# Placing the first projection's products between the transposes of x, and asking for the rotation tables behind the first weights

## The chip, the cores and the metric

The kernel runs on 1 core of one Trainium2 chip. The metric is the device time in microseconds (us) of that core. Before the change, three runs gave a median of 2097.58 us (2097.52 to 2098.06). All names of engines are those of the profile: PE (TensorE, the matrix engine, with PEld for its loads of the stationary operand), DVE (VectorE), ACT (ScalarE), POOL (GpSimd) and SP (SyncE, which issues all DMAs here).

## The reference

One decoder block on x of 2048 rows by 1024 columns, all in float32:

```
h    = rmsnorm(x, norm_g)                         # per row
proj = h @ w_in                                   # 1024 -> 7680 columns
glu_in, conv_gate, q, k, v, attn_gate, merge = split(proj)
c      = silu(layernorm(depthwise_conv31(a * sigmoid(b))))    # a, b = halves of glu_in
y_conv = (c * silu(conv_gate)) @ w_conv_out
q, k   = rope(q), rope(k)                         # rotation by cos, sin tables
y_attn = (window_attention(q, k, v, sinks) * silu(attn_gate)) @ w_attn_out
x      = x + (sigmoid(m1) * y_conv + sigmoid(m2) * y_attn) @ w_out
out    = rmsnorm(x, final_norm_g)
```

The change touches only the very beginning: the norm of the first 1024 rows, their transposes, and the first products with `w_in`.

## The kernel before, in words

The rows are worked in two sweeps of 1024 rows, each sweep in two halves of 512. A sweep projects its rows (`project`), runs the convolution on DVE and the attention beside the projections, and then does the three output products. A float32 product is made of three products in the matrix engine's reduced form: every operand is split in a high part and a remainder ("lo"), and for each of the 8 slices k of the 1024 inputs PE does whi x h-high, whi x h-lo and wlo x h-high ("a triple", 128x512 each), summed in one PSUM bank over 24 products. `load_w` brings a weight tile in two parts (`raw_..0` for k = 0 to 3, `raw_..1` for k = 4 to 7): SP loads `raw`, ACT casts the high part `whi` (line 251), POOL subtracts for `wlo` (line 240).

The start of the first sweep is special. `load_first` asks for four row blocks of x (`xf`, 128x1024 each). `build_h_first` then, for each block, squares and sums it on ACT (line 347), takes a square root on ACT (348), a reciprocal (350) and a scaling of the block (351) on DVE. Then, for each k, it transposes four 128x128 pieces on PE into one PSUM bank `tpf_k` (line 358), copies the high part to `hT_k` on ACT (360) and the remainder on DVE (361). There are three such PSUM banks. `hT_0_k` are the eight tiles of the first half, `hT_1_k` those of the second.

The first items are `gb` and `ga` (the b and the a of glu) and `ka` (a k tile), each first on half 0 and later on half 1. `gb` half 0 is called `mm_gb_000` with weights `whi_gb_000`, `whi_gb_001`. In the kernel before, all of `build_h_first(0)` is run out first, that of half 1 is started on the `Line`, and then the products come. `Line` is the planner of PE's order: `spend(us)` advances a planned time after each triple, and a chain that has yielded `(us, latency)` goes on when its time is due, so that the transposes of half 1 fall between triples.

PE's order is the program's. The order on ACT, DVE, POOL and SP is set by the scheduler of the tile framework, but each of these engines then works its list strictly from the top. The rotation tables `cs` (two loads of 512 KB) are first read by DVE when the first k product is ready (line 457).

Of the kernel before, what the change touches and what calls it, by code (L numbers as in the profile page):

```python
# [52 lines left out]
def hybrid_block(ctx: ExitStack, tc: tile.TileContext, x, par_d, w_in, w_conv, sinks, w_attn, w_out,  # L53
# [16 lines left out]
    def f(ap):  # L70
        return ap.bitcast(F32)
# [8 lines left out]
    def slot(tag, shape, dt, name):  # L80
        n = int(np.prod(shape[1:]))
        full = HALO + T + 2 if tag in WIDE else 1024
        t = slots.tile([P, full], dt, tag=tag, name=name)
        v = t[:, 0:n]
        if len(shape) == 3:
            v = v.rearrange("p (a b) -> p a b", b=shape[2])
        elif len(shape) == 4:
            v = v.rearrange("p (a b c) -> p a b c", b=shape[2], c=shape[3])
        return v
# [11 lines left out]
    def load_first(half):  # L101
        xs = []
        for j in range(4):
            r0 = (4 * half + j) * P
            xs.append(slot(A[7 * half + j], [P, D], F32, f"xf{half}_{j}"))
            nc.sync.dma_start(out=xs[-1], in_=x2[r0:r0 + P, :])
        return xs

    x_first = load_first(0)
# [122 lines left out]
    line = Line()  # L232
# [63 lines left out]
    def make_tiles(tags, half, name):  # L296
        return [slot(tags[half * 8 + k], [P, 2, TH], F32R, f"{name}{half}_{k}") for k in range(KC)]
# [43 lines left out]
    def build_h_first(half, xs):  # L341

        ss = work.tile([P, 2, 4], F32, tag="ss0", name=f"ssf{half}")
        for j in range(4):
            xt = xs[j]
            sq = slot(C[j], [P, D], F32, f"sqf{half}_{j}")
            act.activation(out=sq, in_=xt, func=AF.Square, accum_out=ss[:, 0, j:j + 1])
            act.activation(out=ss[:, 1, j:j + 1], in_=ss[:, 0, j:j + 1], func=AF.Sqrt, bias=eps,
                           scale=1.0 / D)
            dve.reciprocal(out=ss[:, 0, j:j + 1], in_=ss[:, 1, j:j + 1])  # L350
            dve.tensor_scalar(out=xt, in0=xt, scalar1=ss[:, 0, j:j + 1], scalar2=None, op0=ALU.mult)
        yield 0.0, 6.0
        if half == 1:
            ht[1] = make_tiles(h_tags[0], 1, "hT0_")
        for k in range(KC):
            tp = tp_ps.tile([P, 4, P], F32, tag="tp", name=f"tpf{half}_{k}")
            for j in range(4):
                pe.transpose(out=tp[:, j, :], in_=xs[j][:, k * P:(k + 1) * P], identity=ident)
            d = ht[half][k].rearrange("p a (j t) -> p a j t", t=P)
            act.activation(out=d[:, 0], in_=tp, func=AF.Copy, scale=g_norm[:, k, :])  # L360
            dve.scalar_tensor_tensor(out=d[:, 1], in0=tp, scalar=g_norm[:, k, :], in1=f(d[:, 0]),
                                     op0=ALU.mult, op1=ALU.subtract)
            yield 0.44, 0.8

    def program():
        for s in range(NSWEEP):
            yield from sweep(s)

    def sweep(s):
# [36 lines left out]
        def glu_items(c):  # L406
            def ev_b(half, ps):
                if half == 0:
                    glu[c] = slot(glu_slot[c], [P, HALO + T], F32, f"glu{s}_{c}")
                    pool.tensor_copy(out=glu[c][:, 0:HALO], in_=glu_halo[:, c, :])  # L410
                o = HALO + half * TH
                act.activation(out=glu[c][:, o:o + TH], in_=ps, func=AF.Sigmoid)  # L412

            def ev_a(half, ps):
                g = glu[c][:, HALO + half * TH:HALO + (half + 1) * TH]
                dve.tensor_tensor(out=g, in0=ps, in1=g, op=ALU.mult)
                if half == 1:
                    if s + 1 < NSWEEP:
                        pool.tensor_copy(out=glu_halo[:, c, :], in_=glu[c][:, T:T + HALO])
                    line.bg.extend(conv_ops(c))  # L420

            return [project(w_in[C_GLU_B // P + c], h_rhs, f"gb{s}_{c}", ev_b),
                    project(w_in[C_GLU_A // P + c], h_rhs, f"ga{s}_{c}", ev_a)]
# [22 lines left out]
        def load_rope():  # L446
            for half in range(2):
                cs[half] = slot(AT[11 + half], [P, 2, TH], F32, f"cs{s}_{half}")
                t0 = s * T + half * TH
                nc.sync.dma_start(out=cs[half], in_=rope_t[:, :, t0:t0 + TH])  # L450
# [303 lines left out]
        nqkv = len(others)  # L754
        others += gates
        glu_after = list(GLU_AFTER)
        load_rope()
        if s == 0:
            halves = [item[2]() for item in glu_items(0) + others[:1]]
            halves[0][0][0]()  # L760
            xs = load_first(1)
            for _ in build_h_first(0, x_first):
                pass
            line.start(build_h_first(1, xs))
            for half in range(2):
                for i, item in enumerate(halves):
                    yield ((lambda: None) if half == i == 0 else item[half][0],) + item[half][1:]
            glu_after.pop(0)
        for i, item in enumerate(others):
            todo = [item] if s or i else []  # L770
# [183 lines left out]
```

## Time and profile before

| | |
|---|---|
| runs, median (range) | 2097.58 us (2097.52 to 2098.06) |
| profiled execution, its time / its span | 2100.21 us / 2098.5 us |
| busy: PE, PEld, DVE, ACT, POOL | 98%, 80%, 66%, 48%, 23% |
| the chain that ended last, by engine | PE 79%, DVE 11%, DMA 3%, ACT 3%, issue 2%, POOL 1% |
| first transpose / first product / PE without a pause from | 8.41 / 17.84 / 24.93 us |

The execution is a long stretch of PE work, with short waits. The share of PE in the whole span says little on this change, since it acts within the first 45 us only. There one reads the engines' lists in order of time, and asks of each instruction what it waited for.

### The profile page before, as it was taken

How to read it: one execution, taken by the hardware profiler on the slowest of the kernel's cores; microseconds unless marked ns; L12 is line 12 of the kernel's file. 1: busy time of each engine (PE TensorE's matmuls, PEld its weight loads, DVE VectorE, ACT ScalarE, POOL GpSimd, SP SyncE). 2: the span in 40 equal slices, each digit the busy share in tenths (PEclk: the TensorE clock that was granted, in tenths of full speed). 3: DMA queues.
4: the chain of work that ended last, by engine and by line, in shares of the span. 5: the costliest groups of instructions: out<-in, count | busy, mean ns of one | idle time of the engine just before them, and what ended most of it. 6: DMA issues, size and time to landing. Idle time of an engine off the chain costs nothing.

```text
span 2098.5 us, 27434 instructions
## 1 busy us (share of the span) xinstructions
PE 2049.7 (98%) x9256; PEld 1673.3 (80%) x9256; DVE 1394.8 (66%) x1901; ACT 1012.8 (48%) x2251; POOL 477.9 (23%) x336
## 2 busy tenths in 40 slices
PE   7999999999999999999999999999999999999998
PEld 6787887787778877788888888888888888888887
DVE  4979769899988347223558596698889944341224
ACT  6221366665666645112442214767667774521222
POOL 2445432343333322233001121111111110000200
PEclk9999999999999999999999999999999999999999
DMA  7345644554545874646343456555555577574432
GB/s 253 131 141 161 193 145 148 158 164 144 161 138 178 266 231 148 223 136 231 99 151 127 137 178 186 174 172 170 170 156 171 167 228 260 169 233 146 139 122 80
DMA packets 265819, 355.89 MB, mean 170 GB/s; under 512 B 28112, under 2 KB 126544, under 8 KB 265680
## 3 DMA queue, kind: packets, MB, share of 16 engines
q1 hardware_dynamic: 265680, 354.16, 53.1%
q8 instruction: 73, 1.20, 0.3%
q14 instruction: 66, 0.54, 0.1%
HBM read 234.51 MB, written 119.54 MB: 169 GB/s over the span
## 4 chain that ended last, share of the span: by engine, by line
PE 79%; DVE 11%; DMA 3%; ACT 3%; issue 2%; POOL 1%; SPq 1%; DVEq 0%; ACTq 0%; POOLq 0%
PE mm_ma L279 9%; PE o L874 8%; PE mm_yc L279 8%; PE mm_ya L279 7%; PE mm_ag L279 7%; PE mm_gb L279 7%; PE mm_mc L279 7%; DVE cv L390 6%; PE mm_ga L279 6%; PE mm_cg L279 6%; PE mm_q_b L279 3%; PE mm_q_a L279 3%; PE sc L563 2%; PE ov L611 2%; PE mm_v L279 1%
## 5 line engine op out<-in xcount | busy, mean ns | idle before, releaser
L390 DVE SCALAR_TENSOR_TENSOR cv<-glu,par,cv 128x1024 f32<-128x1024 f32 x480 | 682.5, 1422 | 6.3
L602 POOL TENSOR_SCALAR_AFFINE_SELECT pc<-pt 128x1024 fp32r<-128x1024 f32 x60 | 102.4, 1707 | 430.0 <-DVE pt L240 428.2
L874 PE MATMUL o<-wo,mT 128*128 128x512 f32 x768 | 181.3, 394 | 0.0
L874 PEld LDWEIGHTS o<-wo,mT 128*128 128x128 f32 x768 | 143.0, 188 | 32.1
L279 PE MATMUL mm_cg<-hT,whi_cg 128*128 128x512 f32 x512 | 163.3, 400 | 4.5 <-ACT glu L412 2.6
L279 PE MATMUL mm_ma<-hT,whi_ma 128*128 128x512 f32 x512 | 163.2, 400 | 3.9 <-ACT glu L412 3.9
L279 PE MATMUL mm_ga<-hT,whi_ga 128*128 128x512 f32 x512 | 162.5, 399 | 3.5 <-ACT ag L431 2.9
L279 PE MATMUL mm_ya<-aT,whi_ya 128*128 128x512 f32 x512 | 159.1, 392 | 3.4 <-DVE mp L788 3.4
L279 PE MATMUL mm_gb<-hT,whi_gb 128*128 128x512 f32 x512 | 160.8, 395 | 1.5 <-ACT ag L431 1.2
L279 PE MATMUL mm_ag<-hT,whi_ag 128*128 128x512 f32 x512 | 160.9, 395 | 1.2 <-ACT glu L412 1.2
L279 PE MATMUL mm_mc<-hT,whi_mc 128*128 128x512 f32 x512 | 161.1, 396 | 0.0
L279 PE MATMUL mm_yc<-uT,whi_yc 128*128 128x512 f32 x512 | 159.4, 392 | 0.0
L279 PEld LDWEIGHTS mm_ya<-aT,whi_ya 128*128 128x128 f32 x512 | 95.8, 188 | 25.6 <-DVE mp L788 3.1
L279 PEld LDWEIGHTS mm_ga<-hT,whi_ga 128*128 128x128 f32 x512 | 95.1, 190 | 25.3 <-ACT ag L431 3.3
L279 PEld LDWEIGHTS mm_cg<-hT,whi_cg 128*128 128x128 f32 x512 | 95.2, 191 | 25.1 <-ACT glu L412 3.1
L279 PEld LDWEIGHTS mm_ma<-hT,whi_ma 128*128 128x128 f32 x512 | 95.3, 191 | 24.4 <-ACT glu L412 4.3
L279 PEld LDWEIGHTS mm_mc<-hT,whi_mc 128*128 128x128 f32 x512 | 96.7, 189 | 22.4 <-ACT mc L431 0.4
L279 PEld LDWEIGHTS mm_yc<-uT,whi_yc 128*128 128x128 f32 x512 | 96.2, 188 | 21.8
L279 PEld LDWEIGHTS mm_gb<-hT,whi_gb 128*128 128x128 f32 x512 | 94.5, 188 | 22.2 <-ACT ag L431 1.7
L279 PEld LDWEIGHTS mm_ag<-hT,whi_ag 128*128 128x128 f32 x512 | 94.1, 188 | 21.1 <-ACT glu L412 1.6
L581 ACT ACTIVATE ss<-ss,st 128x128 f32<-128x128 f32 x256 | 99.8, 391 | 21.1 <-DVE st L576 20.5
L614 ACT COPY ss<-ov 64x256 f32<-64x256 f32 x128 | 47.0, 367 | 119.9 <-DVE ss L615 97.5
(363 smaller groups left out, 4328.1 us busy)
## 6 DMA issues: line engine op xcount, KB each, us to landing
qk<-d_q SPq DMA_DIRECT2D x256, 64.0 KB, 2.7
d_a<-ss SPq DMA_DIRECT2D x128, 128.0 KB, 1.9
aT<-d_a SPq DMA_DIRECT2D x32, 512.0 KB, 5.9
qk<-d_k SPq DMA_DIRECT2D x240, 64.0 KB, 2.2
raw_gb<-in_w_in_dram SPq DMA_DIRECT2D x34, 256.0 KB, 3.8
raw_ga<-in_w_in_dram SPq DMA_DIRECT2D x34, 256.0 KB, 3.2
raw_ag<-in_w_in_dram SPq DMA_DIRECT2D x32, 256.0 KB, 3.7
d_ag<-ag SPq DMA_DIRECT2D x32, 256.0 KB, 2.4
```

Of the source, the lines that this page charges most:

```text
L279: pe.matmul(out=ps, lhsT=a, rhs=b, start=(k == 0 and i == 0), stop=(k == KC - 1 and i == 2))
L390: dve.scalar_tensor_tensor(out=cv[c], in0=glu[c][:, j:j + T], scalar=tap(c, j), in1=cv[c], op0=ALU.mult, op1=ALU.add)
L563: pe.matmul(out=o, lhsT=q[:, h, :], rhs=r, start=(j == 0), stop=(j == 1))
L581: act.activation(out=sb[:, h, :], in_=sb[:, h, :], func=AF.Exp, scale=SCALE, bias=ngm[:, h:h + 1], accum_out=den[:, h:h + 1])
L602: pool.affine_select(out=pc, in_=f(pt), pattern=[[0, 2], [0, GQ], [1, P]], compare_op=ALU.is_ge, fill=0.0, base=0, channel_multiplier=-1)
L611: pe.matmul(out=ov, lhsT=vv, rhs=pp[:, i % 2], start=(i == 0), stop=(i == nm - 1))
L614: act.copy(oT[own], ovp[other, :, r, :])
L874: pe.matmul(out=ps, lhsT=a[:, c0:c0 + P], rhs=r, start=(k == 0 and i == 0), stop=(k == KC - 1 and i == 2))
```

## The change

Two things. The rotation tables are asked for after the first `gb` weights and the second half's rows, and no longer ahead of them. And for the first half of the rows, the transposes are no longer all done before the first triple: after tiles 0 and 1, one tile's transposes stand between two triples of `gb` (a generator is advanced by one step after each triple). The second half's preparation starts on the planner's line with a delay of 10 instead of 6 planned us.

```
@@ build_h_first
-        yield 0.0, 6.0
+        yield 0.0, 10.0
         if half == 1:
             ht[1] = make_tiles(h_tags[0], 1, "hT0_")
         for k in range(KC):
...
@@ sweep
-        load_rope()
-        if s == 0:
+        if s:
+            load_rope()
+        else:
             halves = [item[2]() for item in glu_items(0) + others[:1]]
             halves[0][0][0]()
             xs = load_first(1)
-            for _ in build_h_first(0, x_first):
-                pass
-            line.start(build_h_first(1, xs))
+            load_rope()
+
+            def first_blocks():
+                gen = build_h_first(0, x_first)
+                for _ in range(3):
+                    next(gen)
+                line.start(build_h_first(1, xs))
+                for us in halves[0][0][1]():
+                    yield us
+                    next(gen, None)
+
             for half in range(2):
                 for i, item in enumerate(halves):
-                    yield ((lambda: None) if half == i == 0 else item[half][0],) + item[half][1:]
+                    yield (lambda: None, first_blocks) if half == i == 0 else item[half]
             glu_after.pop(0)
```

How this stands in the engines' lists. From the 123rd row of PE's list on, and from about the 50th of the other engines', the two kernels' lists are the same.

PE, where tile 2's transposes and the first triple of `gb` meet. Before, tile 7's transposes are followed by the triples one after the other:

```order
L358 MATMUL tpf_7_227<-ident_r,xf_0_80 128x128
L358 MATMUL tpf_7_227<-ident_r,xf_1_82 128x128
L358 MATMUL tpf_7_227<-ident_r,xf_2_84 128x128
L358 MATMUL tpf_7_227<-ident_r,xf_3_86 128x128
L279 MATMUL mm_gb_000_267<-hT_0_0_124,whi_gb_000_139 128x512 x2
L279 MATMUL mm_gb_000_267<-hT_0_0_124,wlo_gb_000_140 128x512
L279 MATMUL mm_gb_000_267<-hT_0_1_125,whi_gb_000_139 128x512 x2
L279 MATMUL mm_gb_000_267<-hT_0_1_125,wlo_gb_000_140 128x512
```

Now, after tile 1's transposes, on the same engine:

```order
L279 MATMUL mm_gb_000_225<-hT_0_0_124,whi_gb_000_135 128x512 x2
L279 MATMUL mm_gb_000_225<-hT_0_0_124,wlo_gb_000_136 128x512
L358 MATMUL tpf_2_229<-ident_r,xf_0_80 128x128
L358 MATMUL tpf_2_229<-ident_r,xf_1_82 128x128
L358 MATMUL tpf_2_229<-ident_r,xf_2_84 128x128
L358 MATMUL tpf_2_229<-ident_r,xf_3_86 128x128
L279 MATMUL mm_gb_000_225<-hT_0_1_125,whi_gb_000_135 128x512 x2
L279 MATMUL mm_gb_000_225<-hT_0_1_125,wlo_gb_000_136 128x512
```

The triple of tile k now stands between the transposes of tile k+1 and those of tile k+2, up to the triple of tile 5; those of tiles 6 and 7 follow without a transpose. The first four transposes of half 1 come after the seventh triple of `ga`, where they came after its first.

ACT, the stretch after its work on the first row blocks. Before (`sqf` with `xf_..149` to `xf_..155` are the squares of half 1's row blocks):

```order
L251 CAST whi_gb_000_139<-raw_gb_000_137 128x512
L251 CAST whi_gb_001_145<-raw_gb_001_143 128x512
L360 ACTIVATE hT_0_4_128<-tpf_4_206,par 128x512
L360 ACTIVATE hT_0_5_129<-tpf_5_213,par 128x512
L360 ACTIVATE hT_0_6_130<-tpf_6_220,par 128x512
L347 ACTIVATE sqf_0_235,ssf_234<-xf_0_149 128x1024
L360 ACTIVATE hT_0_7_131<-tpf_7_227,par 128x512
L348 ACTIVATE ssf_234<-ssf_234,eps_t 128x1
L347 ACTIVATE sqf_1_240,ssf_234<-xf_1_151 128x1024
L347 ACTIVATE sqf_2_245,ssf_234<-xf_2_153 128x1024
L348 ACTIVATE ssf_234<-ssf_234,eps_t 128x1 x2
L347 ACTIVATE sqf_3_250,ssf_234<-xf_3_155 128x1024
```

Now, from the first square of half 1 on (its blocks are here `xf_..145` to `xf_..151`):

```order
L347 ACTIVATE sqf_0_205,ssf_204<-xf_0_145 128x1024
L348 ACTIVATE ssf_204<-ssf_204,eps_t 128x1
L360 ACTIVATE hT_0_2_126<-tpf_2_229,par 128x512
L347 ACTIVATE sqf_1_210,ssf_204<-xf_1_147 128x1024
L360 ACTIVATE hT_0_3_127<-tpf_3_239,par 128x512
L348 ACTIVATE ssf_204<-ssf_204,eps_t 128x1
L347 ACTIVATE sqf_2_215,ssf_204<-xf_2_149 128x1024
L347 ACTIVATE sqf_3_220,ssf_204<-xf_3_151 128x1024
L348 ACTIVATE ssf_204<-ssf_204,eps_t 128x1 x2
L360 ACTIVATE hT_0_4_128<-tpf_4_249,par 128x512
L360 ACTIVATE hT_0_5_129<-tpf_5_260,par 128x512
L251 CAST whi_ga_000_159<-raw_ga_000_157 128x512
```

All four squares of half 1 now stand ahead of `hT_0_4`, where three of them stood behind `hT_0_7`. The two casts of `whi_gb` moved ahead of `hT_0_0`; the casts of `whi_ga` stand between `hT_0_5` and `hT_0_7`. DVE's list follows: three of the four scalings of half 1's blocks stand ahead of the remainder of `hT_0_5`, the fourth right ahead of it.

SP's list of DMA issues. Before:

```order
L135 DMA par<-in_par_dram 128x280
L450 DMA cs_0_133<-in_rope_dram 128x2x512
L450 DMA cs_1_135<-in_rope_dram 128x2x512
L248 DMA raw_gb_000_137<-in_w_in_dram 128x512
L248 DMA raw_gb_001_143<-in_w_in_dram 128x512
L106 DMA xf_0_149<-in_x_dram 128x1024
```

Now, from the same row on:

```order
L135 DMA par<-in_par_dram 128x280
L248 DMA raw_gb_000_133<-in_w_in_dram 128x512
L248 DMA raw_gb_001_139<-in_w_in_dram 128x512
L106 DMA xf_0_145<-in_x_dram 128x1024
L106 DMA xf_1_147<-in_x_dram 128x1024
L106 DMA xf_2_149<-in_x_dram 128x1024
L106 DMA xf_3_151<-in_x_dram 128x1024
L450 DMA cs_0_153<-in_rope_dram 128x2x512
L450 DMA cs_1_155<-in_rope_dram 128x2x512
L248 DMA raw_ga_000_157<-in_w_in_dram 128x512
```

The two tables went behind the second half's rows and still stand ahead of `raw_ga`.

## Rows read from the trace of the kernel before

**Rows 1.** Busy time by stretch: stretch, its length, engines, granted clock, DMA.

```profile
11.09:17.84 6.75, 6.25 (x29) 5.05 (x30) 4.23 (x6) 5.62 (x10) 2.28 (x2) 1.00 1.04 404
17.84:25.60 7.76, 7.12 (x34) 5.30 (x33) 5.81 (x11) 7.73 (x17) 2.23 (x3) 1.00 0.63 241
```

**Rows 2.** PE's list by time: start, us, engine, line, out<-in, count, [idle <-releaser].

```profile
11.09 5.83 PE L358 MATMUL tpf<-ident_r,xf 128*128 128x128 f32 x25 [0.95 <-DVE xf L351]
17.84 0.71 PE L279 MATMUL mm_gb<-hT,whi_gb 128*128 128x512 f32 x2
23.58 0.73 PE L279 MATMUL mm_ga<-hT,whi_ga 128*128 128x512 f32 x2
24.93 0.50 PE L279 MATMUL mm_ga<-hT,wlo_ga 128*128 128x512 f32 x1 [0.62 <-POOL wlo_ga L240]
```

**Rows 3.** Chain of waits, the first 60 us: start, us, what.

```profile
3.72 8.00 DMA cs<-in_rope_dram
...
11.73 8.44 DMA raw_ga<-in_w_in_dram
...
25.43 0.44 PE tpf L358 x4
...
39.37 5.58 PE mm_gb L279 x24
```

**Rows 4.** ACT's list by time, in the columns of rows 2.

```profile
11.60 0.69 ACT L360 ACTIVATE hT<-tpf,par 128x512 fp32r<-128x512 f32 x1 [1.55 <-PE tpf L358]
...
14.87 1.13 ACT L251 CAST whi_gb<-raw_gb 128x512 fp32r<-128x512 f32 x2
15.89 1.85 ACT L360 ACTIVATE hT<-tpf,par 128x512 fp32r<-128x512 f32 x3
17.61 1.07 ACT L347 ACTIVATE sqf<-xf 128x1024 f32<-128x1024 f32 x1
...
18.66 0.70 ACT L360 ACTIVATE hT<-tpf,par 128x512 fp32r<-128x512 f32 x1
...
21.49 0.49 ACT L348 ACTIVATE ssf<-ssf,eps_t 128x1 f32<-128x1 f32 x2
...
22.90 0.62 ACT L251 CAST whi_ga<-raw_ga 128x512 fp32r<-128x512 f32 x1
```

**Rows 5.** SP's list of issues, and below it par's time to landing.

```profile
3.23 0.44 SPq L135 DMA_DIRECT2D par<-in_par_dram  x1
...
DMA to landing us min/median/max: 6.8/6.8/6.8
```

**Rows 6.** The transposes alone, in two stretches: count, ns min/median/max, from, to.

```profile
L358 PE MATMUL tpf<-ident_r,xf x7: 417/417/417, 13.6 to 14.9; 128*128 128x128 f32 x7
...
L358 PE MATMUL tpf<-ident_r,xf x3: 272/273/332, 17.4 to 17.7; 128*128 128x128 f32 x3
```

**Rows 7.** A later wait, PE's list by time.

```profile
197.78 1.08 PE L279 MATMUL mm_q_b<-hT,whi_q_b 128*128 128x512 f32 x2 [3.43 <-DVE rb_q__1_1524 L464]
...
199.09 1.06 PE L279 MATMUL mm_q_b<-hT,whi_q_b 128*128 128x512 f32 x2
...
200.37 1.06 PE L279 MATMUL mm_q_b<-hT,whi_q_b 128*128 128x512 f32 x2
```

**Rows 8.** The same stretch by windows: length, PE busy, granted clock, DMA.

```profile
198.00:201.00 3.00, 3.00 (x8) 0.50 0.47 158
202.00:204.00 2.00, 2.00 (x10) 1.00 0.82 244
```

**Rows 9.** DVE's list by time: remainders of hT, and scalings of half 1's blocks.

```profile
16.62 2.07 DVE L361 SCALAR_TENSOR_TENSOR hT<-tpf,par,hT 128x512 fp32r<-128x512 f32 x3 [0.86 <-ACT hT L360]
...
22.03 0.75 DVE L351 TENSOR_SCALAR xf<-xf,ssf 128x1024 f32<-128x1024 f32 x1
...
23.95 1.48 DVE L351 TENSOR_SCALAR xf<-xf,ssf 128x1024 f32<-128x1024 f32 x1
```

**Rows 10.** POOL's list by time.

```profile
23.60 2.98 POOL L240 TENSOR_TENSOR wlo_ga<-raw_ga,whi_ga 128x512 fp32r<-128x512 f32 x2 [5.53 <-ACT whi_ga L251]
```

## The prediction

> **What bounds the kernel now.** I read the busy time by stretch first, then the lists of PE, ACT, DVE, POOL and SP over the first 45 us, then the chain of waits. PE bounds the kernel, but not before 25 us. It transposes from 11.09 and starts the first triple only at 17.84 [rows 2]. In that stretch of 6.75 us PE looks busy (6.25) and ACT has 5.62; in the next, 7.76 us long, ACT has 7.73: there ACT's list never stops [rows 1]. PE waits a last time in this start for `wlo_ga`, whose cast stands on ACT behind three squares of half 1 (22.90, [rows 4]): the first two products of `ga` run from 23.58, the third only from 24.93 [rows 2]. So the start is bound by ACT as much as by PE, and the question for the change is when ACT delivers the tiles `hT`.
>
> Since the lists of all engines agree after the first 45 us, I take a delay at the end of the start as passed on in full: in the chain, PE's work follows without a gap from 25.43 to `gb` at 39.37 [rows 3].
>
> **The prices.** A triple costs 5.58 / 8 = 0.70, one tile's four transposes 0.44 beside triples [rows 3]. ACT, from start to start: a high part 0.58 ((1.85 - 0.69) / 2), a pair of casts 1.02 (14.87 to 15.89), a square with its read-out 1.05 (17.61 to 18.66), a root 0.2 [rows 4]. A high part is ready after 0.7. DVE: a remainder 0.66 from one to the next, ready after 0.75; a scaling 0.75 [rows 9].
>
> PE's early work costs more. The transposes take 417 ns each up to 14.9 and start 0.21 apart (7 in 1.3 us), so 0.85 per tile; after 17.4 they take 273 [rows 6]. The granted clock in the rows reads 1.00 in both stretches [rows 1], so it doesn't show this. It does at 198: after a wait of 3.43 us PE runs at 0.50 of its 2.4 GHz, and a triple takes 200.37 - 199.09 = 1.28 instead of 0.70; later it is 1.00 again [rows 7, 8]. I take 1.2 GHz from the first transpose to about 17, as before, since PE starts at the same 11.09 and has about as much to do.
>
> The Trainium skill, "TensorE: Matmul & The Clock Gate" (What's actually happening), says that half rate is the state in which PE starts, and that activity lifts it; the durations agree with that, the granted clock of the first rows doesn't.
>
> **The tables behind the weights.** `par` lands at 3.23 + 6.8 = 10.03 [rows 5]. The first table, 512 KB, landed next, at 3.72 + 8.00 = 11.72 [rows 3]. Now the two `raw_gb` parts, 512 KB together, stand there: I take 10.9 and 11.7. Earliest would be both at about 10.0 to 10.5, latest as before, when the casts began at 14.87 [rows 4]. The second half's blocks come 1 MB earlier, some 2.6 us at 400 GB/s [rows 1]; `raw_ga` has the same bytes ahead of it, and keeps its 11.73 + 8.44 = 20.2 [rows 3]. `cs` is read by DVE only after the first `ka`, past 35 us: its later landing, below 20, costs nothing.
>
> **The transposes and triples, step by step** (PE, then ACT and DVE where they are late):
> - Casts at 10.9 and 11.7, then `hT_0_0` at 12.2 (11.60 before, [rows 4]), ready 12.9, and `hT_0_1` at 12.8, the first square at 13.35.
> - Triple 0 starts at 12.93, waits for its remainder (13.7), and ends at 14.6: 4.9 us earlier than triple 0 did (17.84 plus its length). This is the gain of the change. Transposes of tile 2 to 15.4, triple 1 to 16.7, tile 3 to 17.6, all at half clock.
> - ACT: `hT_0_2` at 15.7, second square 16.3, `hT_0_3` 17.85, root, third square 18.6, fourth 19.7, two roots, and only then `hT_0_4` at 21.1. Here the gain goes back: before, `hT_0_4` stood at 15.89 [rows 4].
> - PE has triples 2 and 3 and the transposes of tiles 4 and 5 done at 20.25, and idles until 21.84. DVE makes the remainder of tile 4 at 22.05 to 22.8, behind the scaling of the third block. Triple 4 ends 23.3, tile 6 is transposed by 23.7, triple 5 waits for its remainder (24.2) and ends 24.6, tile 7's transposes end at 25.1.
> - `hT_0_7` at 25.26 (18.66 before), its remainder at 26.76, and triple 7 ends at 27.2. With three PSUM banks and two tiles of lead, each triple from the fourth on pays for part of the round from PE to ACT to DVE and back.
> - The first triple of `ga` follows with no wait (its casts at 22.3 and 24.5, POOL done by 24.4 with the first, 1.49 each [rows 10]), to 27.9.
>
> Before, PE had `gb`, the first triple of `ga` and four transposes of half 1 behind it at 24.93 + 0.23 + 0.44 = 25.60 [rows 2, 3]. The same work is done at 27.9 + 0.44 = 28.35. That is +2.75 us. The table loads and `glu` on ACT lie behind this and beside PE's `ga`: hidden. The transposes of half 1's last three tiles now fall between triples of `gb` half 1; the last triple there comes 1.4 us after the last transposes, whose high part and remainder take 0.3 + 0.7 + 0.75: about 0.2 more. Sum +2.95.
>
> On the profiled execution this is 2100.21 + 2.95 = 2103.2. It stood 2.63 above the median of the runs, which gives **2100.5 us**.
>
> Bounds of the unknown: by the same list, weights at 10.0 to 10.5 give +2.3, weights and blocks of half 1 as late as before +4.6; full clock from the start +1.5, half clock to the end of this `gb` +5.7.
>
> **A lock that may add to it.** The fourth scaling took 1.48 instead of 0.75 when it started at 23.95 behind a POOL subtraction begun at 23.60 [rows 9, 10]. Now it starts at 22.7 and POOL's first subtraction for `ga` at 22.9: a race by 0.2. If POOL is first, the scaling waits for POOL's 24.4, and the remainders of tiles 5 to 7 with it: +1.4. If DVE is first, nothing.
>
> The Trainium skill, "SBUF — State Buffer" (SBUF: two separate sides), calls the port pair that VectorE and GpSimd share an exclusive lock, held for a whole instruction. The row of 1.48 agrees. By this rule the sum is +2.95 or +4.35, by who comes first.
>
> **Rivals.**
> 1. *The interleave pays* (faster). ACT is early with every tile, and PE never waits from 11.09 on. For: PE idles in both stretches, and the first triple starts 4.9 us earlier. PE would need 33 transposes and 27 products, 8.25 x 0.44 + 9 x 0.70 = 9.9, and 2.7 more for the 5.4 us at half clock: done at 23.7, against 25.6. That is -1.9: 2095.7, at the very best. Against: the squares ahead of `hT_0_4` in ACT's list. It decides whether `hT_0_4` starts before about 17.5.
> 2. *Nothing moves* (within 0.5 of 2097.6). The wait for `ga`'s weights goes, the one for `hT` comes, and both are of a size. For: ACT's total work up to `glu` is the same in both kernels. Against: before, ACT's work for half 1 lay beside triples that had all they needed; now triples wait behind it.
> 3. *POOL takes the lock first*: +4.35, 2101.9. By the times above DVE is first by 0.2, which is less than I can place.
> 4. *The clock stays at half* through the first `gb`, since PE now has gaps: +5.7, 2103.3. Against: the gaps in my list are below 2 us, and the fall in the later stretch followed 3.43 us of idleness [rows 7, 8].
>
> By the page on the clock gate an idle stretch takes PE back to half rate; that rule would lead to rival 4, if the gaps were long enough.
>
> **How the numbers follow.** Forecast (2099.3 to 2101.5) 0.53, rival 1 0.10, rival 2 0.14, rival 3 0.15, rival 4 0.08. A measurement can tell about 0.2%, or 4.2 us, from no change. Rival 1 doesn't reach that at its best, so faster gets 0.02, for what I have not seen. Slower by more than 4.2 us needs 2101.8: rival 4, most of rival 3, and a little of the forecast's tail with late weights, 0.23. The rest, 0.75, is no difference. Range: from 2098.0, which takes in part of rival 2, to 2102.8, past rival 3 and short of rival 4.
>
> **What would show it.** In the profile after: the `whi_gb` casts from 10.9 to 12.3; the first triple's start near 12.9; `hT_0_4` on ACT at about 21, behind four squares; PE waiting for `hT` of ACT and DVE several times between 17 and 27, and no longer for `wlo_ga`; the first `ga` triple at about 27. The fourth scaling's time, 0.75 or 1.48, decides rival 3; transposes of 273 ns or of 417 ns after 18 decide rival 4. I am wrong if `hT_0_4` comes early, if the `raw_gb` parts land after 13, or if a wait after 45 us, where the lists agree, grows or shrinks by more than 1 us.

## The result, and the profile after

| | before | after |
|---|---|---|
| median of 20 runs each (range) | 2097.27 us (2095.51 to 2099.85) | 2100.49 us (2098.09 to 2102.95) |
| profiled execution, time / span | 2100.21 / 2098.5 us | 2102.25 / 2100.5 us |
| 4th row block's first transpose | 11.09 us | 12.03 us |
| first product of `ga` | 23.58 us | 28.68 us |
| first product of `kb` | 55.96 us | 60.18 us |

The ratio is 1.0017, 95% interval 1.001 to 1.0023: 3.2 us slower, where +2.9 was forecast.

Two times serve as marks below: the start of the first transpose that reads the fourth row block, which waits for nothing of the change, and the start of the first `kb` product, behind everything that the change touches. The distance between them I call the **start length**. It is 44.87 us before and 60.18 - 12.03 = 48.15 after, +3.28.

PE's list of the kernel after, in the columns of rows 2:

```profile
12.03 1.33 PE L358 MATMUL tpf<-ident_r,xf 128*128 128x128 f32 x5 [0.89 <-DVE xf L351]
13.28 1.58 PE L279 MATMUL mm_gb<-hT,whi_gb 128*128 128x512 f32 x2
...
15.79 0.93 PE L279 MATMUL mm_gb<-hT,whi_gb 128*128 128x512 f32 x2
...
19.32 0.50 PE L279 MATMUL mm_gb<-hT,whi_gb 128*128 128x512 f32 x1 [0.21 <-DVE hT L361]
...
21.74 0.50 PE L279 MATMUL mm_gb<-hT,whi_gb 128*128 128x512 f32 x1 [1.24 <-ACT hT L360]
22.68 0.50 PE L279 MATMUL mm_gb<-hT,whi_gb 128*128 128x512 f32 x1 [0.45 <-DVE hT L361]
...
23.36 1.05 PE L358 MATMUL tpf<-ident_r,xf 128*128 128x128 f32 x4
24.07 1.20 PE L279 MATMUL mm_gb<-hT,whi_gb 128*128 128x512 f32 x2
...
25.49 1.05 PE L358 MATMUL tpf<-ident_r,xf 128*128 128x128 f32 x4
...
28.11 0.50 PE L279 MATMUL mm_gb<-hT,whi_gb 128*128 128x512 f32 x1 [0.29 <-DVE hT L361]
...
28.68 0.63 PE L279 MATMUL mm_ga<-hT,whi_ga 128*128 128x512 f32 x2
...
48.12 0.82 PE L279 MATMUL mm_gb<-hT,whi_gb 128*128 128x512 f32 x2
```

The first triple starts 4.56 us earlier than before [rows 2], and `ga` starts 5.10 later. Between them PE's list names waits for `hT`, from ACT (1.24) and from DVE (0.21, 0.45, 0.29), and none for `wlo_ga`.

ACT's list of the same stretch:

```profile
11.35 1.29 ACT L251 CAST whi_gb<-raw_gb 128x512 fp32r<-128x512 f32 x2 [0.36 <-DMA raw_gb<-in_w_in_dram]
...
13.98 1.05 ACT L347 ACTIVATE sqf<-xf 128x1024 f32<-128x1024 f32 x1
...
16.18 0.69 ACT L360 ACTIVATE hT<-tpf,par 128x512 fp32r<-128x512 f32 x1 [0.73 <-PE tpf L358]
...
18.56 1.05 ACT L347 ACTIVATE sqf<-xf 128x1024 f32<-128x1024 f32 x1
...
19.60 1.05 ACT L347 ACTIVATE sqf<-xf 128x1024 f32<-128x1024 f32 x1
...
20.64 0.47 ACT L348 ACTIVATE ssf<-ssf,eps_t 128x1 f32<-128x1 f32 x2
21.01 1.25 ACT L360 ACTIVATE hT<-tpf,par 128x512 fp32r<-128x512 f32 x2
...
24.45 0.69 ACT L360 ACTIVATE hT<-tpf,par 128x512 fp32r<-128x512 f32 x1 [1.69 <-PE tpf L358]
```

The casts are 3.5 us earlier than in [rows 4]. `hT_0_4` could be made from about 18.9 us on (PE's transposes of tile 4 ran from 18.28 for 0.60), but stands behind two squares and two roots until 21.01. After that ACT waits for PE, 1.69 us: the work now goes round PE, ACT and DVE one step at a time.

The windows of after, the same two stretches as in rows 1:

```profile
11.09:17.84 6.75, 5.79 (x22) 4.11 (x22) 4.01 (x7) 5.50 (x11) 2.52 (x2) 1.00 1.03 411
17.84:25.60 7.76, 5.87 (x24) 4.08 (x25) 4.96 (x10) 6.07 (x14) 1.58 (x1) 0.84 0.68 256
```

In the second, PE is busy for 5.87 us where it was 7.12, and 0.84 is new: the granted clock fell to one half, 1.2 GHz, at 23.1, behind the waits that end at 21.74 and 22.68. The triple at 24.07 takes 25.49 - 24.07 = 1.42 us instead of 0.70.

The chain of waits of after (start, us, what):

```profile
18.66 2.08 ACT sqf L347 x4
...
27.31 0.76 DVE hT L361
...
28.84 4.79 PE mm_ga L279 x21
...
46.88 2.29 PE mm_gb L279 x9
```

Squares of half 1 now lie on the chain, ahead of products of half 0. From 28.84 on PE has no gap up to `kb` but a small one at the last triple of `gb` half 1: from 46.88 on, 9 products take 2.29 us where three triples take 2.09, and in PE's list the pair at 48.12 takes 0.82 instead of 0.62.

### The profile page after: what moved, and what is told of

Read it like the earlier page. It is cut to its first block, busy times and chain, and to the rows that moved or that the text cites. A ratio compares the mean times of both kernels' runs of the same rounds, so it can differ in the third digit from the quotient of the medians.

```text
span 2100.5 us, 27432 instructions
## 1 busy us (share of the span) xinstructions
PE 2051.2 (98%) x9256; PEld 1673.9 (80%) x9256; DVE 1392.5 (66%) x1901; ACT 1013.5 (48%) x2251; POOL 477.5 (23%) x336
## 4 chain that ended last, share of the span: by engine, by line
PE 78%; DVE 14%; ACT 3%; DMA 2%; issue 2%; POOL 0%; SPq 0%; DVEq 0%; ACTq 0%; POOLq 0%
PE mm_ma L279 9%; PE o L883 8%; PE mm_yc L279 8%; DVE cv L390 8%; PE mm_ya L279 7%; PE mm_ag L279 6%; PE mm_gb L279 6%; PE mm_mc L279 6%; PE mm_ga L279 6%; PE mm_cg L279 6%; PE mm_q_b L279 3%; PE mm_q_a L279 3%; PE sc L563 2%; PE ov L611 2%; PE mm_v L279 1%
```

## The experiments

The theory: the interleave loses because half 1's squares stand ahead of `hT_0_4` on ACT, where triples now wait for it; the load order gains by itself. The rivals: the load order is what costs; the round from PE to ACT to DVE costs, whatever stands on ACT; the difference is chance.

All start lengths (from profiles, one execution each) and medians:

| kernel | 4th block | first `kb` | start length | against 44.87 | median (range, runs) | ratio, 95% |
|---|---|---|---|---|---|---|
| before | 11.09 | 55.96 | 44.87 | | see each ratio | |
| before again | 12.09 | 56.95 | 44.86 | -0.01 | 2096.02 (1) | |
| after | 12.03 | 60.18 | 48.15 | +3.28 | 2100.49 (20) | 1.0017 [1.001, 1.0023] |
| after again | 11.52 | 59.37 | 47.85 | +2.98 | 2100.24 (1) | |
| load order alone | 11.91 | 55.61 | 43.70 | -1.17 | 2096.37 (2093.72 to 2097.74, 11) | 0.9995 [0.9987, 1.0004] |
| interleave alone | 12.21 | 63.63 | 51.42 | +6.55 | 2104.21 (2103.18 to 2107.4, 5) | 1.0038 [1.0025, 1.005] |
| half 1 started later | 11.34 | 57.02 | 45.68 | +0.81 | 2098.28 (2096.2 to 2099.27, 11) | 1.0004 [0.9995, 1.0013] |
| after, no squares of half 1 | 11.96 | 56.38 | 44.42 | -0.45 | 2098.21 (2097.07 to 2098.71, 10) | 1.0005 [0.9996, 1.0014] |
| before, no squares of half 1 | 11.74 | 55.44 | 43.70 | -1.17 | 2095.76 (2095.0 to 2098.14, 10) | 0.9998 [0.9988, 1.0007] |

The first four experiments ran with 27 runs of before, median 2096.92; the last with 13, median 2096.87. By the medians only after and the interleave alone are clear of before; what sets the other kernels apart is read from the start lengths, which agree to 0.01 and 0.30 us where a kernel was profiled twice.

**Load order alone.** The transposes are left as before.

```
-        load_rope()
-        if s == 0:
+        if s:
+            load_rope()
+        else:
...
             xs = load_first(1)
+            load_rope()
```

> Marker: the start of the first kb product on PE, 55.96 us in the profile before and 60.18 after; from there on all lists agree. This kernel has the new order of the loads alone, and all transposes ahead of the first triple as before. Theory A (the cost is the round PE-ACT-DVE in which triples wait behind the squares of half 1): with no triple between transposes nothing is lost; the whi_gb casts come before hT_0_0, and the marker is at 55.0 to 56.5, the time that of before within 1.5 us. Theory B (the cost is the order of the loads, which lets the third row block land a microsecond late and bunches the second half's rows with the weights): marker 58.5 or later, time at least 2 us above before.

PE's list:

```profile
23.89 0.61 PE L279 MATMUL mm_ga<-hT,whi_ga 128*128 128x512 f32 x2
24.58 0.50 PE L279 MATMUL mm_ga<-hT,wlo_ga 128*128 128x512 f32 x1
```

The third product of `ga` starts 0.69 us behind the first, where before had 1.35 with its wait of 0.62 [rows 2]. The first `kb` product at 55.61 is theory A's. The order of the loads costs nothing: it shortens the start by 1.17 us. The time, 0.55 us below before, is too small for the interval.

**Interleave alone.** The tables stay ahead of the weights, all else is the change.

```
-        if s:
-            load_rope()
-        else:
+        load_rope()
+        if s == 0:
...
-            load_rope()
```

> The new place of the triples alone, with the rotation tables asked for ahead of the weights as before. Theory A: triples wait behind the squares as in the change, and the weights land some 3 us later on top: worked out with the durations of the profile before, the marker (first kb product) is at 61 to 62.5, later than with both parts (60.18), the time 3.5 to 6 us above before. Theory B: marker 57 or earlier, time within 1.5 us of before.

PE's list:

```profile
14.81 1.22 PE L279 MATMUL mm_gb<-hT,whi_gb 128*128 128x512 f32 x2 [1.28 <-ACT whi_gb L251]
...
26.77 0.51 PE L279 MATMUL mm_gb<-hT,whi_gb 128*128 128x512 f32 x1 [2.28 <-ACT hT L360]
27.91 0.80 PE L279 MATMUL mm_gb<-hT,whi_gb 128*128 128x512 f32 x1 [0.64 <-DVE hT L361]
```

A window of the same kernel, in the columns of rows 1:

```profile
28.00:31.00 3.00, 3.00 (x9) 2.38 (x10) 1.73 (x3) 0.69 (x1) 1.96 (x2) 0.50 0.68 201
```

The direction is theory A's, the size lies above its range, by the first `kb` product (63.63) and by the time (7.3 us above before): the wait for the weights' casts is added, the one for `hT` is 2.28 instead of 1.24, and half clock follows it again. Of the two parts of the change the interleave loses, and the load order gives back 51.42 - 48.15 = 3.3 of it.

**Half 1 started later.** The change, with half 1's preparation put on the planner's line after the last triple of `gb`, and its planned delay shortened so that PE's list stays that of after.

```
-        yield 0.0, 10.0
+        yield 0.0, 10.0 if half == 0 else 4.6
...
-                line.start(build_h_first(1, xs))
                 for us in halves[0][0][1]():
                     yield us
                     next(gen, None)
+                line.start(build_h_first(1, xs))
```

> Both parts of the change, but the preparation of half 1 (squares, roots, scalings) is started in the program after the eight triples of gb; the scheduler then puts hT_0_4 and hT_0_5 ahead of the fourth square on ACT, and both casts of whi_ga behind hT_0_7. PE's list is that of the change. Theory A: hT_0_4 comes 1 to 2 us earlier, the marker is at 56.5 to 58.5, the time 0.5 to 2.5 above before. Theory B: marker 60 to 60.5 as with the change, for the loads stand in the same order.

ACT's list:

```profile
18.27 1.04 ACT L347 ACTIVATE sqf<-xf 128x1024 f32<-128x1024 f32 x1
...
19.31 0.67 ACT L360 ACTIVATE hT<-tpf,par 128x512 fp32r<-128x512 f32 x1
```

PE's list of the same kernel:

```profile
20.82 0.50 PE L279 MATMUL mm_gb<-hT,whi_gb 128*128 128x512 f32 x1 [0.28 <-DVE hT L361]
...
23.99 0.50 PE L279 MATMUL mm_gb<-hT,whi_gb 128*128 128x512 f32 x1 [0.57 <-DVE hT L361]
...
25.27 0.63 PE L279 MATMUL mm_ga<-hT,whi_ga 128*128 128x512 f32 x2
```

`hT_0_4` now stands behind three squares instead of four, is at 19.31, and PE's wait for ACT there is gone; no wait is longer than 0.57. The window from 17.84 to 25.60 has a granted clock of 1.00. The start is 2.47 us shorter than after's (2.17 by the second profile of after): theory A.

**After, without half 1's squares.** Half 1's blocks are scaled with half 0's factors, so the squares, roots and reciprocals of half 1 are left out of the output.

```
-            sq = slot(C[j], [P, D], F32, f"sqf{half}_{j}")
-            act.activation(out=sq, in_=xt, func=AF.Square, accum_out=ss[:, 0, j:j + 1])
+            if half == 0:
+                sq = slot(C[j], [P, D], F32, f"sqf{half}_{j}")
+                act.activation(out=sq, in_=xt, func=AF.Square, accum_out=ss[:, 0, j:j + 1])
...
```

> The change, with the squares, roots and reciprocals of half 1 left out (its rows are scaled by half 0's factors): the four squares are gone from ACT's list, so that nothing but the casts of whi_gb stands between the tiles hT. Theory A: PE no longer idles for hT_0_4, the first ga product starts at 25 to 26 instead of 28.68, and the marker is at 56 to 57.5. Theory B: marker 59 to 60.2. If the third row block again starts its square about a microsecond later than in the profile before (8.14 against 7.15), that lateness belongs to the order of the loads and not to chance.

PE's list:

```profile
15.02 0.78 PE L363 MATMUL tpf<-ident_r,xf 128*128 128x128 f32 x4
...
18.29 0.89 PE L279 MATMUL mm_gb<-hT,whi_gb 128*128 128x512 f32 x2
...
19.60 1.00 PE L279 MATMUL mm_gb<-hT,whi_gb 128*128 128x512 f32 x2
...
24.14 0.50 PE L279 MATMUL mm_gb<-hT,whi_gb 128*128 128x512 f32 x1 [0.29 <-DVE hT L366]
...
24.71 0.62 PE L279 MATMUL mm_ga<-hT,whi_ga 128*128 128x512 f32 x2
```

ACT's list of the same kernel:

```profile
15.84 0.69 ACT L365 ACTIVATE hT<-tpf,par 128x512 fp32r<-128x512 f32 x1 [1.83 <-PE tpf L363]
```

Theory A's again: the start is 3.73 us shorter than after's (3.43 by the second profile of after), and `ga` starts at 24.71, sooner even than the 25 to 26 expected. What is left are short waits for remainders, most of them seen as pairs that take 0.9 to 1.0 instead of 0.62.

Not all of the 3.4 to 3.7 need be the squares'. The half clock of the first transposes ended sooner in this execution: those of tile 2 take 0.78, in after 1.05. `hT_0_2` starts 15.84 - 11.96 = 3.88 us behind the mark, in the two profiles of after 4.15 and 4.28, and it waits for PE in all three, not for a square. So 0.3 to 0.4 us may be chance.

**Before, without half 1's squares.** The same edit on the kernel before, as a control.

> The kernel before, without the squares, roots and reciprocals of half 1 (half 1's blocks are scaled with half 0's factors, so that part is left out of the output). It is the control for the change without these squares, which started the first kb product at 56.38 us, 3.80 us ahead of the change as made (60.18). The kernel before starts it at 55.96. Theory A (the squares cost only where triples wait behind them on ACT): in the order of before they lie beside triples, and PE gains little more than the waits of 0.62 and 0.2 for ga's weights: first kb product at 54.8 to 55.6. The interleave without squares then costs 0.8 to 1.6. Theory B (ACT's work of about 4.8 us for half 1 is on the path in either order, and the interleave itself is what costs 4): first kb product at 51.5 to 53.5.

PE's list:

```profile
24.05 0.61 PE L279 MATMUL mm_ga<-hT,whi_ga 128*128 128x512 f32 x2
24.50 0.40 PE L279 MATMUL mm_ga<-hT,wlo_ga 128*128 128x512 f32 x1
```

Theory A: 55.44. The squares cost 44.87 - 43.70 = 1.17 in the order of before, and 3.4 to 3.7 in the interleaved one. Taking them away leaves the two orders 44.42 - 43.70 = 0.72 apart, perhaps up to 1.1 without the early clock just named: that much is the round between the engines, the rest is ACT's order and the clock that falls behind its wait. These two kernels differ in the load order too. But the load order alone, with the loads of after, has the same 43.70 with all squares done, so nearly all of them are hidden there. That the two are equal is chance: its third product of `ga` comes 0.24 later behind the first than here (0.69 against 0.45), and its first triple 0.33 sooner behind the mark (6.43 against 6.76).

**The change again.**

> The change once more, unaltered, to see what of the 60.18 us to the first kb product varies from run to run. In the first profile the third row block's square began at 8.14 us, and the granted clock fell to half at 23.1 for 3.4 us. Theory A (both are chance, and the lists' effect is about the +2.95 forecast): with the third square near 7.2 and no fall at 23, the first kb product starts at 58.7 to 59.4; with the late square alone at 59.4 to 60.0. Theory B (late block and fall belong to the change): both are seen again, and the product starts at 60.0 to 60.4.

PE's list:

```profile
11.52 1.33 PE L358 MATMUL tpf<-ident_r,xf 128*128 128x128 f32 x5 [0.89 <-DVE xf L351]
...
21.36 0.49 PE L279 MATMUL mm_gb<-hT,whi_gb 128*128 128x512 f32 x1 [1.25 <-ACT hT L360]
22.30 0.50 PE L279 MATMUL mm_gb<-hT,whi_gb 128*128 128x512 f32 x1 [0.46 <-DVE hT L361]
...
27.85 0.63 PE L279 MATMUL mm_ga<-hT,whi_ga 128*128 128x512 f32 x2
```

A window of the same execution:

```profile
23.00:27.00 4.00, 4.00 (x16) 2.92 (x14) 1.86 (x3) 2.44 (x5) 2.32 (x2) 0.57 0.19 74
```

Neither theory as it was put. The third row block's square begins at 7.64, late by half as much, and 59.37 lies in theory A's first range; but that range was given for no fall of the clock, and the waits of 1.25 and 0.46 and the fall are there again. So the fall goes with the change in both profiles, the late row block does not.

**The kernel before again.**

> The kernel before once more. In its first profile the third row block's square began at 7.15 us, the first kb product at 55.96, and the granted clock fell to half at 785 us, which none of the other kernels showed. Theory A (the fall at 785 is chance, and with it 3 to 3.7 us of that execution's time): no fall at 785 here, and the span shorter than 2098.5 by 1 to 4 us, the first kb product at 55.7 to 57.0, later if the third square is late. Theory B (the fall belongs to the kernel before): it is seen again at 785, and the span is 2098 to 2099.

PE's list of this second profile:

```profile
12.09 5.78 PE L358 MATMUL tpf<-ident_r,xf 128*128 128x128 f32 x25 [0.89 <-DVE xf L351]
...
25.93 0.50 PE L279 MATMUL mm_ga<-hT,wlo_ga 128*128 128x512 f32 x1 [0.62 <-POOL wlo_ga L240]
```

The fourth block is 1.00 us later than in the first profile, and the start length agrees to 0.01. So the block's arrival (11.09 to 12.21 over nine profiles, in every load order) is chance, and adds itself to the start as it is. The third square, at 8.20 here and at 8.07 in after without half 1's squares, is late under either load order, so the lateness is not the loads'. The span is 4.2 us shorter, 2094.3, a little more than the 1 to 4 expected. Where, a row of PE's list of the first profile of before shows:

```profile
784.44 0.51 PE L655 MATMUL lnvar<-vsumh,ones 128*128 128x512 f32 x1 [1.80 <-ACT mc L431]
```

The window behind that row, of the same first profile:

```profile
785.00:788.00 3.00, 3.00 (x9) 2.31 (x7) 1.58 (x1) 2.97 (x4) 0.00 (x0) 0.50 0.88 287
```

The same window of the second profile:

```profile
785.00:788.00 3.00, 3.00 (x14) 2.46 (x14) 3.00 (x3) 1.53 (x2) 0.00 (x0) 1.00 0.35 118
```

The wait of 1.80 and the half clock behind it are missing in the repeat. Theory A: chance. With the 1.6 us that after loses at 98 us (below), it is the reason why the two spans of before and after differ by 2.0 only, although their first `kb` products differ by 4.2.

## Why the prediction was right

Its mechanism is the one that the runs show, and its sum, +2.95, is close to the start lengths, +3.28 and +2.98, and to the medians, +3.2. By its steps, times counted from the fourth block's first transpose:

- *Weights and first triple.* The casts came at 11.35, between the values taken; the triple at 1.25 us from the mark (1.84 forecast; 1.37 in the second profile).
- *`hT_0_4` behind four squares.* At 8.98 us (10.0 forecast). ACT was earlier because PE was: the pair at 15.79 took 0.93, on its way from 1.20 to 0.71, so half clock ended near 16, 4 us behind the mark, and not near 17, 6 behind it.
- *PE's waits.* PE's list names one for ACT and three for DVE, the longest 1.24, where 20.25 to 21.84, 1.59, was forecast. The wait for `wlo_ga` is gone.
- *From the end of that wait to `ga`.* 28.68 - 21.74 = 6.94 us (6.49 in the second profile), where 21.84 to 27.2, 5.36, was forecast. This term was mis-sized by 1.1 to 1.6, and by its cause: **the fall of the clock**. The two tiles' transposes took 0.71 instead of 0.36 each and the triple 1.42 instead of 0.70, 1.4 together. Rival 4 was given 0.08 because the gaps were below 2 us; the fall came behind waits of 1.24 and 0.45, here and in the repeat. So rival 4 came in part: some 3 us at half clock, not the whole of `gb`.
- These two errors, about 1.0 too late up to the wait and 1.1 to 1.6 too little behind it, had opposite signs. That the total is better than its parts is luck.
- *The last triples of half 1, +0.2.* Right: the pair at 48.12 takes 0.82 instead of 0.62. The total doesn't show it, since the triples of `ga` that have no transposes between them take 0.68 instead of 0.70, and other small differences make up the rest. By `ga` with its first triple and a tile's transposes the start is 28.68 + 0.70 + 0.44 - 12.03 = 17.79, against 14.51 before: the same +3.28 as at `kb`.
- *Bounds.* Late weights were put at +4.6; with the tables first it was +6.55. Half clock followed the longer wait there too; how much of the 6.55 is its doing, no run shows.

The rivals. Rival 1 (the interleave pays) was said to hang on `hT_0_4`. That was too kind to it: with no squares of half 1 at all the interleave is 0.72 behind the other order. Rival 2 failed as forecast: the wait for `ga`'s weights went, but what came for it was larger. Rival 3 did not occur; DVE came first. DVE's list of after:

```profile
22.55 0.74 DVE L351 TENSOR_SCALAR xf<-xf,ssf 128x1024 f32<-128x1024 f32 x1
```

POOL's list of after:

```profile
22.84 1.58 POOL L240 TENSOR_TENSOR wlo_ga<-raw_ga,whi_ga 128x512 fp32r<-128x512 f32 x1 [8.27 <-ACT whi_ga L251]
25.73 1.28 POOL L240 TENSOR_TENSOR wlo_ga<-raw_ga,whi_ga 128x512 fp32r<-128x512 f32 x1 [1.31 <-ACT whi_ga L251]
```

The scaling keeps its 0.74, and POOL's subtraction, begun 0.29 later, takes 1.58 instead of 1.28. In [rows 9, 10] POOL was first, and the scaling took 1.48. The Trainium skill, "SBUF — State Buffer" (SBUF: two separate sides), gives the pair of ports to whichever starts first; both orders here agree in who was held up. The subtraction grew by 0.30 only, where 0.45 of the scaling was left when it began.

One condition did not hold: a wait where the lists agree shrank by more than 1 us, the one for `mc`, 1.80 in before. PE's list of after:

```profile
788.46 0.50 PE L655 MATMUL lnvar<-vsumh,ones 128*128 128x512 f32 x1 [0.57 <-ACT mc L431]
```

It is not the change's: the second profile of before doesn't have the wait at all. A second place moved without its wait. After has half clock at 98.4 to 101.4, 3 us in which before ran at full clock; PE's wait in front of it is the same (2.18 and 2.20). It costs 1.6 of that execution. It isn't the change's either: the second profile of after has 1.00 there, and the load order alone has 0.50.

What stays open: no experiment gave the interleave more than two tiles of lead, and none held the clock up through the wait, so the 3.4 to 3.7 us are not split between the wait and the clock by a run, only by rows.

## What to carry to other kernels

When products are moved forward between the steps that prepare their operands, look first at the engine that makes those operands: every instruction ahead of them in its list, however harmless beside products that have all they need, then stands on the path. Undo a mixed change part by part: here, by the start lengths, the load order gained 1.2 us by itself, and the interleave put on top of it lost 4.2 to 4.5. And to compare starts of a few us, measure from the last event that varies by chance: with that, two profiles of one kernel agreed to 0.01 and 0.3 us, while their spans differed by up to 4.2.

## What the runs showed of the hardware

- Half clock follows waits shorter than I had taken: at 23 us, behind 1.24 and 0.45 us in one profile of after, 1.25 and 0.46 in the other. It doesn't always follow a longer one: behind one and the same wait of 2.1 to 2.2 us for `vs`, at 92 to 101 us, the granted clock was 0.50 in five of nine profiles and 1.00 in four. The Trainium skill, "TensorE: Matmul & The Clock Gate" (What's actually happening), has the clock set by how busy PE has lately been; the falls agree with that, and no run here shows what decided between the five and the four.
- The first half clock did not last equally long: the transposes of tile 2, at 15 us in both, took 1.05 in after, as they did behind the fall at 23.1, and 0.78 in after without half 1's squares. The granted clock in the rows reads 1.00 there in both.
- The fourth row block's first transpose came at 11.09 to 12.21 us in nine profiles, and 1.00 us apart in two profiles of one kernel.
